# Half-size products for the last four groups of an input projection, PSUM banks 6 and 2, stores on two queues

## The chip, the cores and the metric

The kernel runs on one core of a Trainium2 chip. The metric is the device time of one execution in microseconds (us); lower is better. Five engines work side by side: TensorE (PE, matrix products), VectorE (DVE), ScalarE (ACT), GpSimd (POOL) and SyncE (SP, which here only issues DMA transfers). An engine runs its instructions in order; an instruction that waits for another engine holds up all that stands behind it on its own.

## The reference, cut to what matters

One encoder layer over a sequence of 2048 positions and 2048 channels, in float32:

```python
h = rms_norm(x, norm_g) * (1 + scale) + shift            # scale, shift, gate from silu(c) @ w_ada
z = h @ w_in + b_in                                      # 2048 x 2048 @ 2048 x 4096: input projection
u_pool, u_lru, g_pool, g_lru = z[:, :1024], z[:, 1024:2048], z[:, 2048:3072], z[:, 3072:]
y_pool = pool_mixer(u_pool, ...)                         # 4 groups of 256 channels: window sums, then a 256 x 256 product
y_lru = bidir_rg_lru(conv(u_lru), ...)                   # 4 heads of 256 channels: gate products, a scan in each direction
y = concat(rms_norm(y_pool) * silu(g_pool), rms_norm(y_lru) * silu(g_lru)) @ w_out + b_out   # output projection
out = rms_norm(x + gate * y, final_norm_g)
```

## The kernel before

**Steps.** The program is a loop over steps `t`. A step is 24 matmuls of 128x128 by 128x512 (line 310): each of four output banks of 128x512 gets 256 rows of the contraction, and each float32 product is made of three products of split operands (`mm3`: high by high, high by low, low by high). Step `t` has a moving tile `m` (the split of a raw tile of 128x2x512 floats, made by ACT and DVE two steps ahead in `m_split`, lines 169 and 170) and a stationary tile `s`.

**Stages.** Steps 0 to 255 are the input projection: eight groups (four "L" heads, four "P" pool groups) of four blocks of 512 positions, eight steps a block. After a block ACT moves its four banks out of PSUM (`evac`, line 449): two to the group's `u` tiles in SBUF, two to a raw tile `gr`, which is stored to DRAM. Steps 256 to 367 are the output projection, in two halves of 56 steps. Each half is a 2 by 2 block product made of seven products of half size instead of eight (Strassen's way in Winograd's form): sums and differences of blocks are multiplied (`PRODUCTS`), and the results are added up in `out_evac`. The differences of the moving side (`T1` to `T4`, out of `w_out`) are made ahead by `combine` and kept in DRAM; those of the stationary side are made in `unit_split`.

**Work beside the steps.** The units of the groups (`lru_unit`: convolution, gate products on PE, sigmoid, scan, merge; `pool_unit`: window sums, product, gating) are put at steps by the tables `L_START` and `P_START`; their products use the banks `px`. All else (the 48 rows of `w_ada`, `combine`, row norms, final rows) is put at steps by `at`. A scheduler then orders each engine's instructions within narrow bounds; an engine's order is fixed when the program is built.

**Buffers.** PSUM has eight banks: five `pm` for the projections, three `px` for all else (in the output projection every second block takes three `px` and one `pm`). Raw tiles of 512 KB rotate through eight buffers (`raw_p`): a load into one waits until the tile that was handed out eight earlier is done with. Eight `s` buffers hold stationary tiles, three hold moving tiles, eight `big` ones hold `u` tiles and others. SP issues all loads and stores, in order (`load`, `store`).

Of the kernel before, what the change touches and what calls it, by code (L numbers as in the profile page):

```python
# [13 lines left out]
D = 2048  # L14
S = 2048
# [29 lines left out]
def layer(ctx: ExitStack, tc: tile.TileContext, xc, xn, c, wada, win, wgate, wpool, wout, vecs, consts, bout, fng, out):  # L45
# [3 lines left out]
    s_p = pool("s", 8)  # L49
# [7 lines left out]
    ps_m = pool("ps_m", 5, space=bass.MemoryType.PSUM)  # L57
    ps_x = pool("ps_x", 3, space=bass.MemoryType.PSUM)
# [45 lines left out]
    sscr = [dram.tile([128, 2, TB], F32, name=f"ss{p}") for p in range(4)]  # L104
# [28 lines left out]

    def wout_src(name, p, q):
        k = int(name[1:])
        if name[0] == "T":
# [38 lines left out]
    def modulate(t):  # L175
# [10 lines left out]
        store(out=xscr[tb][p], in_=r)  # L186
# [91 lines left out]
    def normed(r, sg, h, k, p):  # L278
        for j in range(2):
            vtt(out=r[:, j], in0=r[:, j], in1=rn_t[2 * sg + h, "PL"[k]], op=ALU.mult)  # L280
        late.append((yscr[PAIRS[p + 4 * k]][2 * sg + h], r))
        if (sg, h, p) == (0, 1, 3):
            del rn_t[1, "PL"[k]], rn_t[0, "PL"[k]]

    def unit_split(u):
# [16 lines left out]
        s = s_p.tile([128, 2, 2, TB], F32R, tag="s", name="s")  # L302
# [132 lines left out]
    def evac_fix(g, tb):  # L435
# [5 lines left out]
        store(out=gscr[g][tb], in_=gr)  # L441

    def evac(g, tb, banks):
# [6 lines left out]
        store(out=gscr[g][tb], in_=gr)  # L450
# [32 lines left out]
    def lru_unit(g, h, d, tb, b, last):  # L483
# [48 lines left out]
        def scan():  # L532
# [21 lines left out]
            if d == 0:  # L554
                store(out=hscr[h][tb], in_=st["h"])
# [486 lines left out]
```

## Time and profile before

| | before |
|---|---|
| median of 3 runs | 2274.55 us (2274.26 to 2274.68) |
| profiled execution: time, span | 2274.88 us, 2272.7 us |
| PE busy | 2241.9 us, 9832 matmuls |
| DVE, ACT busy | 1656.3 us, 1294.4 us |
| data moved | 533.55 MB, mean 235 GB/s |

The span is the time from the first instruction to the last as the profiler saw it; the profiled execution's own time is 2.18 us longer. A busy time is the union of an engine's instructions. A PE that waits inside a row of matmuls can be shown as busy, so matmuls are also counted by stretch. "Idle before" is an engine's waiting time ahead of a group of instructions, with what ended it.

### The profile page before, as it was taken

The numbers are of one execution on the slowest core, as the hardware profiler recorded it, in microseconds if no ns is written. First come the engines' busy times: TensorE is split into PE (matmuls) and PEld (weight loads), VectorE is DVE, ScalarE is ACT, GpSimd is POOL, SyncE is SP. The second block draws the span as 40 slices with busy tenths as digits, with TensorE's granted clock in tenths as the row PEclk, the third lists the DMA queues.
The fourth block names the chain that finished last, engine by engine and source line by source line (L and its number), as shares of the span: only waits on it lengthen the run. The fifth ranks groups of instructions, "written<-read, shape, count | busy, mean of one in ns | idle before, by whom it ended". The sixth has DMA issues, their size and how long they took to land.

```text
span 2272.7 us, 26096 instructions
## 1 busy us (share of the span) xinstructions
PE 2241.9 (99%) x9832; PEld 1845.5 (81%) x9832; DVE 1656.3 (73%) x1986; ACT 1294.4 (57%) x1609; POOL 6.2 (0%) x40
## 2 busy tenths in 40 slices
PE   7999999999999999999999999999999999999996
PEld 6888888888888888888888888887788888888885
DVE  7999677478867564677675657668976668977579
ACT  4555677576755666666667467678643333443332
POOL 0000000000000000000000000000000000000000
PEclk9999999999999999999999999999999999999998
DMA  9878766445956654674466446654787657897555
GB/s 390 330 281 334 262 218 225 178 158 202 342 184 235 241 180 172 213 245 158 168 251 238 176 171 228 233 200 168 268 306 277 216 192 241 318 364 259 187 177 203
DMA packets 139455, 533.55 MB, mean 235 GB/s; under 512 B 15424, under 2 KB 16704, under 8 KB 131392
## 3 DMA queue, kind: packets, MB, share of 16 engines
q1 hardware_dynamic: 139328, 531.88, 65.1%
q8 instruction: 77, 1.26, 0.2%
q14 instruction: 50, 0.41, 0.1%
HBM read 417.52 MB, written 114.29 MB: 234 GB/s over the span
## 4 chain that ended last, share of the span: by engine, by line
PE 95%; DVE 3%; DMA 1%; issue 0%; ACT 0%; SPq 0%; DVEq 0%
PE pm L310 75%; PE px L310 20%; DVE o L775 1%; DMA ada<-in_wada_dram 1%; DMA xr<-in_xc_dram 0%; PE px L393 0%; DVE sqP L395 0%; DVE m L170 0%; DVE o L754 0%; DVE o L753 0%; DVE sqL L395 0%; DVE o L725 0%; PE px L707 0%; DVE x L746 0%; DVE th L549 0%
## 5 line engine op out<-in xcount | busy, mean ns | idle before, releaser
L310 PE MATMUL pm<-m,s 128*128 128x512 f32 x7674 | 1771.0, 390 | 0.0
L310 PEld LDWEIGHTS pm<-m,s 128*128 128x128 f32 x7674 | 1440.8, 188 | 304.0 <-issue 4.1
L169 ACT ACTIVATE m<-xr 128x1024 fp32r<-128x1024 f32 x366 | 386.4, 1056 | 587.0 <-PE pm L310 396.8
L170 DVE TENSOR_TENSOR m<-xr,m 128x1024 fp32r<-128x1024 f32 x366 | 446.2, 1219 | 359.8 <-ACT m L169 348.1
L310 PE MATMUL px<-m,s 128*128 128x512 f32 x1134 | 270.7, 392 | 13.8 <-ACT m L359 12.4
L310 PEld LDWEIGHTS px<-m,s 128*128 128x128 f32 x1134 | 213.6, 189 | 60.3 <-ACT m L359 12.4
L310 PE MATMUL px<-uch,gw 128*128 128x512 f32 x768 | 186.8, 391 | 0.0
L310 PEld LDWEIGHTS px<-uch,gw 128*128 128x128 f32 x768 | 144.3, 188 | 31.5 <-ACT sqL L394 0.5
L378 DVE CUSTOM_DVE_ANT_0 ada<-ada,cact 128x2048 f32<-128x2048 f32 x47 | 107.4, 2285 | 11.7 <-DMA ada<-in_wada_dram 11.7
L520 DVE TENSOR_TENSOR ig<-ig,u 128x512 f32<-128x512 f32 x64 | 44.1, 689 | 58.7 <-ACT ig L518 58.7
L303 ACT ACTIVATE s<-yr 128x1024 fp32r<-128x1024 f32 x56 | 59.0, 1053 | 46.3 <-DVE yr L299 21.8
L539 DVE SCALAR_TENSOR_TENSOR th<-rg,th 128x512 f32<-128x512 f32 x64 | 42.5, 683 | 51.7 <-ACT th L534 51.3
L304 DVE TENSOR_TENSOR s<-yr,s 128x1024 fp32r<-128x1024 f32 x56 | 68.2, 1218 | 12.3 <-ACT s L303 12.2
L235 DVE TENSOR_TENSOR s<-wr,s 128x1024 fp32r<-128x1024 f32 x56 | 68.1, 1215 | 1.0 <-ACT s L234 1.0
L185 ACT ACTIVATE xr<-xr,shv 128x512 f32<-128x512 f32 x64 | 44.3, 719 | 34.2 <-DVE xr L184 29.5
L755 ACT ACTIVATE x<-o 128x1024 f32<-128x1024 f32 (+1 forms) x36 | 34.7, 965 | 50.6 <-DVE o L754 49.1
L234 ACT ACTIVATE s<-wr 128x1024 fp32r<-128x1024 f32 x56 | 58.6, 1046 | 3.8 <-PE pm L310 2.0
L504 ACT ACTIVATE uch<-u 128x512 fp32r<-128x512 f32 x64 | 38.8, 626 | 37.3 <-DVE u L499 37.2
L253 DVE TENSOR_TENSOR tr<-tr 128x1024 f32<-128x1024 f32 x32 | 39.1, 1221 | 22.3 <-DMA tr<-in_wout_dram 21.3
L518 ACT ACT_TABLE_LOAD x42 | 53.9, 1283 | 0.7
L499 DVE SCALAR_TENSOR_TENSOR cv<-u,vec,cv 128x512 f32<-128x512 f32 x64 | 45.8, 743 | 6.7 <-ACT cv L497 6.7
L518 ACT ACTIVATE ig<-px,vec 128x512 f32<-128x512 f32 x64 | 43.7, 683 | 10.7 <-PE px L310 10.2
(161 smaller groups left out, 1658.3 us busy)
## 6 DMA issues: line engine op xcount, KB each, us to landing
xr<-xs SPq DMA_DIRECT2D x192, 512.0 KB, 5.4
ada<-in_wada_dram SPq DMA_DIRECT2D x47, 1024.0 KB, 6.9
yr<-ys SPq DMA_DIRECT2D x88, 512.0 KB, 4.7
wr<-in_win_dram SPq DMA_DIRECT2D x71, 512.0 KB, 6.0
xr<-t SPq DMA_DIRECT2D x64, 512.0 KB, 4.4
xr<-in_xc_dram SPq DMA_DIRECT2D x63, 512.0 KB, 6.3
tr<-in_wout_dram SPq DMA_DIRECT2D x48, 512.0 KB, 4.7
xr<-in_wout_dram SPq DMA_DIRECT2D x48, 512.0 KB, 4.7
```

The costliest lines, as they stand in the source:

```text
L169: act(out=m[:, 0], in_=r, func=AF.Copy)
L170: vtt(out=m[:, 1], in0=r, in1=mf[:, 0], op=ALU.subtract)
L185: act(out=r[:, j], in_=r[:, j], func=AF.Identity, bias=shv[:, k:k + 1])
L234: act(out=s[:, 0], in_=r, func=AF.Copy)
L235: vtt(out=s[:, 1], in0=r, in1=sf[:, 0], op=ALU.subtract)
L303: act(out=s[:, 0], in_=r, func=AF.Copy)
L304: vtt(out=s[:, 1], in0=r, in1=s.bitcast(F32)[:, 0], op=ALU.subtract)
L310: nc.tensor.matmul(out=ps, lhsT=a[:, x, j, asl], rhs=b[:, y, j], start=first and i == 0, stop=last and i == 2, skip_group_check=more)
L378: nc.vector.tensor_tensor_reduce(out=t, in0=t, in1=cact["t"], op0=ALU.mult, op1=ALU.add, scale=1.0, scalar=0.0, accum_out=mod[:, i:i + 1])
L499: stt(out=a if k < 3 else U[i][:, us], in0=src, scalar=cw, in1=a, op0=ALU.mult, op1=ALU.add)
L518: act(out=v, in_=st.pop(("ps", w, i)), func=AF.Sigmoid, bias=V("b_gate", (d * 4 + h) * 4 + 2 * w + i))
L520: vtt(out=st["i", i], in0=st["i", i], in1=U[i][:, us], op=ALU.mult)
```

## The change

Steps 128 to 255 of the input projection (its last four groups) become 112 steps: two supergroups `sg` 0 and 1 of two groups each, every one made of seven half-size products like the output projection. The output projection is now `sg` 2 and 3, and the program has 352 steps. The order of groups 4 and 5 is swapped, and the columns of `w_in` are laid out accordingly.

- `combine` runs for both projections: 32 differences of blocks of the normalised input (`xscr`) go to `hcomb` at steps 66 to 138, 32 of `w_out` to `tscr` at steps 138 to 233.
- `unit_split` makes the stationary sums for all four supergroups; `S2` now stores two tiles (`sscr[0]`, `sscr[1]`), so `S3` needs no subtraction.
- `in_evac` adds up the seven products of the input projection, mostly on DVE straight from PSUM, in `u` and two `sum` tiles; `evac` stays for groups 1 to 3.
- Product 1 is chained onto product 0 in the same banks (and 6 onto 5) only in `sg` 3; in `sg` 2 that sum is made by DVE in `out_evac`.
- PSUM: six `pm` banks and two `px`. `s` tiles: six, and two more (`sx`) up to step 128; from there the space holds the `sum` tiles.
- Stores of `modulate` and `evac` are issued by ACT (`act_store`); `hscr`, `yscr`, `gscr` and `tscr` stores go through the list `late`, which SP issues at the next step, after that step's loads.
- The unit tables (`L_AT`, `P_AT`), the loads of final rows and the norms are put at other steps.

```diff
-GROUPS = [("L", 0), ("P", 3), ("L", 1), ("L", 2), ("P", 2), ("L", 3), ("P", 1), ("P", 0)]
+GROUPS = [("L", 0), ("P", 3), ("L", 1), ("L", 2), ("L", 3), ("P", 2), ("P", 1), ("P", 0)]
...
-    s_p = pool("s", 8)
+    s_p = pool("s", 6)
...
-    ps_m = pool("ps_m", 5, space=bass.MemoryType.PSUM)
-    ps_x = pool("ps_x", 3, space=bass.MemoryType.PSUM)
+    last_p = {"p": tc.alloc_tile_pool(name="sx", bufs=2)}
+    ps_m = pool("ps_m", 6, space=bass.MemoryType.PSUM)
+    ps_x = pool("ps_x", 2, space=bass.MemoryType.PSUM)
...
+    act_store = nc.scalar.dma_start
...
-    NT1 = 256
+    T1 = 128
     SG = 56
+    NT1 = T1 + 2 * SG
     NT = NT1 + 2 * SG
...
-        store(out=xscr[tb][p], in_=r)
+        act_store(out=xscr[tb][p], in_=r)
...
-        store(out=gscr[g][tb], in_=gr)
+        act_store(out=gscr[g][tb], in_=gr)
...
+    def in_evac(sg, k, q, banks):
...
+            if k == 0:
+                act(out=hi, in_=ps, func=AF.Copy)
+            elif k == 1:
+                stt(out=lo, in0=ps, scalar=bu, in1=hi, op0=ALU.add, op1=ALU.add)
+            elif k == 2:
+                vtt(out=hi, in0=ps, in1=hi, op=ALU.add)
+            elif k == 3:
+                vtt(out=U3[q][:, n], in0=ps, in1=hi, op=ALU.add)
+            elif k == 4:
...
+                stt(out=g_t[g, q][:, i], in0=U3[q][:, n], scalar=bg_, in1=ps, op0=ALU.add, op1=ALU.subtract)
...
+            elif k == 5:
+                stt(out=U3[q][:, n], in0=ps, scalar=bg_, in1=U3[q][:, n], op0=ALU.add, op1=ALU.add)
+                vtt(out=hi, in0=ps, in1=hi, op=ALU.add)
...
+            else:
+                stt(out=hi, in0=ps, scalar=bu, in1=hi, op0=ALU.add, op1=ALU.add)
...
-            store(out=yscr[g][tb], in_=gr)
+            late.append((yscr[g][tb], gr))
...
+            more = sg == 3 and k in CHAINED
+            key = (8 + sg, CHAINED[k] if more else k, q)
...
-                banks[key] = [px(), px(), px(), pm()] if t >= NT1 and q else [pm() for _ in range(4)]
+                banks[key] = [px(), px(), pm(), pm()] if t >= T1 and sg == 3 and q else [pm() for _ in range(4)]
```

What this does to the queues is shown at three places. First, the end of a block of the input projection. Before, ACT copies the four banks (`u_...` and `gr` from `pm`), here in the third group:

```order
L449 ACTIVATE u_3381<-pm,vec 128x512
L449 ACTIVATE u_3384<-pm,vec 128x512
L449 ACTIVATE gr<-pm,vec 128x512 x2
L169 ACTIVATE m<-xr 128x1024 x3
L518 ACT_TABLE_LOAD
```

Now, in the second half of the input projection, DVE does it; here the sixth product of `sg` 0 (k = 5, q = 0), with the moving tile's split (L180) ahead:

```order
L180 TENSOR_TENSOR m<-xr,m 128x1024
L608 SCALAR_TENSOR_TENSOR th<-rg,carry,ig 128x512
L504 SCALAR_TENSOR_TENSOR sum<-pm,vec,sum 128x512
L505 TENSOR_TENSOR u_6662<-pm,u_6662 128x512
L504 SCALAR_TENSOR_TENSOR sum<-pm,vec,sum 128x512
L505 TENSOR_TENSOR u_6665<-pm,u_6665 128x512
L504 SCALAR_TENSOR_TENSOR sum<-pm,vec,sum 128x512
L505 TENSOR_TENSOR u_6668<-pm,u_6668 128x512
L504 SCALAR_TENSOR_TENSOR sum<-pm,vec,sum 128x512
L505 TENSOR_TENSOR u_6671<-pm,u_6671 128x512
L626 TENSOR_TENSOR hl<-hl,th 128x512 x2
```

The reading of the banks has moved from ACT to DVE, and at this product it is eight instructions instead of four. Second, SP's queue in the third group. Before, the stores of `gr` and `hf` stand between the loads of moving tiles (`xr`):

```order
L154 DMA xr<-xs_3_229 128x1024
L555 DMA hs_0_138<-hf 128x1024
L154 DMA xr<-xs_4_230 128x1024
L154 DMA xr<-xs_5_231 128x1024
L450 DMA gs_0_114<-gr 128x1024
L154 DMA xr<-xs_6_232 128x1024
```

Now the store of `gr` is issued by ACT, and SP has the loads and stores of the differences (`tr`, `h_...`) instead:

```order
L164 DMA xr<-xs_5_262 128x1024
L1017 DMA hs_1_142<-hf 128x1024
L269 DMA tr<-h_1_0_227 128x1024
L269 DMA tr<-xs_5_262 128x1024
L164 DMA xr<-xs_6_263 128x1024
L164 DMA xr<-xs_7_264 128x1024
L269 DMA tr<-h_1_1_228 128x1024
L269 DMA tr<-xs_5_270 128x1024
L164 DMA xr<-xs_0_265 128x1024
L1017 DMA h_1_0_243<-tr 128x1024
```

The store that waits for a block's end has left SP's queue, and up to three other transfers stand between two loads of moving tiles. Third, PE early in the input projection, around the gate products of an L unit (`px<-uch,gw`), which come in two halves of 12. Before:

```order
L310 MATMUL px<-uch,gw 128x512 x12
L310 MATMUL pm<-m,s 128x512 x24
L310 MATMUL px<-uch,gw 128x512 x12
L310 MATMUL pm<-m,s 128x512 x120
```

Now:

```order
L334 MATMUL px<-uch,gw 128x512 x6
L334 MATMUL pm<-m,s 128x512 x18
L334 MATMUL px<-uch,gw 128x512 x6
L334 MATMUL pm<-m,s 128x512 x106
L334 MATMUL px<-uch,gw 128x512 x12
```

With two `px` banks a half fills both, so the next half needs both of them read; in some places the scheduler has put 18 matmuls of a step between the two products of a half.

## Rows read from the trace of the kernel before

**Rows 1.** The page: busy us (share) and instructions; the granted clock by slice.

```profile
PE 2241.9 (99%) x9832; PEld 1845.5 (81%) x9832; DVE 1656.3 (73%) x1986; ACT 1294.4 (57%) x1609; POOL 6.2 (0%) x40
...
PEclk9999999999999999999999999999999999999998
```

**Rows 2.** The page: the chain that ended last, by engine.

```profile
PE 95%; DVE 3%; DMA 1%; issue 0%; ACT 0%; SPq 0%; DVEq 0%
```

**Rows 3.** PE in order of time: start us, us, what, count [idle before].

```profile
12.38 3.96 PE L310 MATMUL px<-m,s 128*128 128x512 f32 x9 [12.38 <-ACT m L359]
...
2254.41 1.56 PE L310 MATMUL pm<-ml,s 128*128 128x512 f32 x6
```

**Rows 4.** Groups by form: names, shapes, count | busy us, mean ns | idle before, releaser.

```profile
L310 PE MATMUL pm<-m,s 128*128 128x512 f32 x7674 | 1771.0, 390 | 0.0
...
L170 DVE TENSOR_TENSOR m<-xr,m 128x1024 fp32r<-128x1024 f32 x366 | 446.2, 1219 | 359.8 <-ACT m L169 348.1 <-DMA gwr<-in_wgate_dram 6.5 <-DMA gl<-gs 4.3
L169 ACT ACTIVATE m<-xr 128x1024 fp32r<-128x1024 f32 x366 | 386.4, 1056 | 587.0 <-PE pm L310 396.8 <-issue 150.9 <-DMA xr<-in_wout_dram 10.2
L310 PE MATMUL px<-m,s 128*128 128x512 f32 x1134 | 270.7, 392 | 13.8 <-ACT m L359 12.4 <-DVE m L170 0.7 <-ACT s L364 0.5
...
L304 DVE TENSOR_TENSOR s<-yr,s 128x1024 fp32r<-128x1024 f32 x56 | 68.2, 1218 | 12.3 <-ACT s L303 12.2
...
L303 ACT ACTIVATE s<-yr 128x1024 fp32r<-128x1024 f32 x56 | 59.0, 1053 | 46.3 <-DVE yr L299 21.8 <-DVE yr L280 10.7 <-DVE yr L296 9.4
...
L253 DVE TENSOR_TENSOR tr<-tr 128x1024 f32<-128x1024 f32 x32 | 39.1, 1221 | 22.3 <-DMA tr<-in_wout_dram 21.3 <-DMA tr<-t 0.8 <-issue 0.2
...
L449 ACT ACTIVATE u<-pm,vec 128x512 f32<-128x512 f32 x56 | 37.1, 680 | 11.6 <-PE pm L310 11.5
...
L299 DVE TENSOR_TENSOR yr<-yr 128x1024 f32<-128x1024 f32 x16 | 19.5, 1221 | 15.5 <-DMA yr<-ss 9.1 <-DMA yr<-ys 6.4
...
L725 DVE TENSOR_TENSOR o<-pm,o 128x512 f32<-128x512 f32 x20 | 13.1, 684 | 3.6 <-PE pm L310 3.5
```

**Rows 5.** The chain in order of time: start us, us, what.

```profile
297.67 27.21 PE pm L310 x120
```

**Rows 6.** Stretches: us, length, busy (count) by engine, clock, DMA share, GB/s.

```profile
0.00:60.00 60.00, 46.87 (x197) 37.87 (x198) 48.39 (x62) 27.92 (x32) 0.44 (x6) 1.00 0.99 391
120.00:180.00 60.00, 60.00 (x262) 49.00 (x261) 59.94 (x86) 34.04 (x37) 0.00 (x0) 1.00 0.87 329
...
660.00:720.00 60.00, 60.00 (x266) 49.67 (x265) 40.86 (x48) 35.51 (x45) 0.00 (x0) 1.00 0.52 190
...
1920.00:1980.00 60.00, 60.00 (x266) 49.73 (x265) 59.46 (x68) 25.87 (x38) 0.00 (x0) 1.00 0.82 293
1980.00:2040.00 60.00, 60.00 (x266) 49.69 (x266) 46.11 (x48) 22.81 (x29) 0.00 (x0) 1.00 0.97 364
```

**Rows 7.** The same for steps 88 to 95, and for steps 128 to 255.

```profile
543.03:597.78 54.75, 54.75 (x241) 44.94 (x240) 48.96 (x65) 46.20 (x58) 0.28 (x4) 1.00 0.83 299
...
799.28:1637.81 838.53, 838.28 (x3675) 689.37 (x3674) 561.23 (x701) 554.18 (x685) 0.83 (x12) 1.00 0.58 205
```

**Rows 8.** Waits of SP's queue: who waited for whom, us, times, longest us.

```profile
SPq L450 <- ACT gr L449: 181.8, 26, 19.7
SPq L154 <- DVE m L170: 157.0, 53, 10.1
```

**Rows 9.** The page: DMA issues by form, count, KB each, median us to landing.

```profile
xr<-xs SPq DMA_DIRECT2D x192, 512.0 KB, 5.4
```

**Rows 10.** ACT around one L unit's first gate products, in order of time.

```profile
736.55 0.69 ACT L518 ACTIVATE rg<-px,vec 128x512 f32<-128x512 f32 x1
737.14 0.68 ACT L518 ACTIVATE ig<-px,vec 128x512 f32<-128x512 f32 x1
```

**Rows 11.** PE at the same place.

```profile
736.66 5.61 PE L310 MATMUL pm<-m,s 128*128 128x512 f32 x24
742.11 2.89 PE L310 MATMUL px<-uch,gw 128*128 128x512 f32 x12
```

More of the change, by code (lines that the diff above doesn't have):

```diff
@@ L156, in m_load @@
             sg, k, q, p = where2(t)
-            load(out=r, in_=wout_src(PRODUCTS[k][1], p, q))
+            load(out=r, in_=moving("in" if sg < 2 else "out", PRODUCTS[k][1], p, q))
         xraw[t] = r
@@ L554, in scan @@
             if d == 0:
-                store(out=hscr[h][tb], in_=st["h"])
+                late.append((hscr[h][tb], st["h"]))
         def reload():
@@ L650, in fin @@
                 vtt(out=v, in0=v, in1=y, op=ALU.add)
-            store(out=yscr[g][tb], in_=gr)
+            late.append((yscr[g][tb], gr))
         at(b, sums)
@@ L731, in out_evac @@
                 vtt(out=b[:, hi], in0=ps, in1=b[:, hi], op=ALU.add)
+                if not sg:
+                    vtt(out=a[:, hi], in0=ps, in1=a[:, hi], op=ALU.add)
     x_t = {}
@@ L736, in row_of, with x_pair @@
         return 8 * sg + n
+    def x_pair(sg, n):
+        t = big("x")[:, :D].rearrange("p (i t) -> p i t", i=2)
+        i = row_of(sg, n)
+        for k in range(2):
+            load(out=t[:, k], in_=xn[(i + k) * 128:(i + k + 1) * 128, 1024:])
+            x_t[sg, n + k, 1] = t[:, k]
     def x_load(sg, n, h):
@@ L863, in start_unit, with rn_load, rn @@
             pool_unit(g, GROUPS[g][1], tb, b, last)
-    rn_at = [(244, 1, "L"), (244, 2, "L"), (245, 3, "L"), (245, 0, "P"), (249, 1, "P"), (250, 0, "L"), (254, 2, "P"), (259, 3, "P")]
+    def rn_load(tb, kind):
+        r = raw("rq")
+        load(out=r, in_=qscr[kind][tb])
+        rn_t[tb, kind] = r
+    def rn(tb, kind):
+        if "rn" not in fin:
+            fin["rn"] = big("rn")[:, :4 * TB].rearrange("p (i t) -> p i t", i=4)
+        r = rn_t[tb, kind]
+        v = rn_t[tb, kind] = fin["rn"][:, 2 * (tb % 2) + (kind == "L")]
+        ps = px()
+        vtt(out=r[:, 0], in0=r[:, 0], in1=r[:, 1], op=ALU.add)
+        nc.tensor.matmul(out=ps, lhsT=ones, rhs=r[:, 0], start=True, stop=True)
+        act(out=v, in_=ps, func=AF.Sqrt, scale=2.0 / S, bias=epsc)
+        nc.vector.reciprocal(out=v, in_=v)
+    rn_at = [(228, 0, "P"), (229, 0, "L"), (230, 1, "L"), (231, 2, "L"), (232, 3, "L"), (242, 1, "P"), (248, 2, "P"), (254, 3, "P")]
     def rn(tb, kind):
@@ L922, in layer @@
             sg, k, q, p = where2(t)
-            key = (8 + sg, CHAINED.get(k, k), q)
+            more = sg == 3 and k in CHAINED
+            key = (8 + sg, CHAINED[k] if more else k, q)
             sk = (8 + sg, PRODUCTS[k][0])
-            first, last = p == 0 and k not in CHAINED, p == 3
+            first, last = p == 0 and not more, p == 3
+        e = t + W_AHEAD - 25
+        if 0 <= e < 96 and e % 32 < 8:
+            w_load(e // 32 + 1, e % 32)
+        if t + W_AHEAD in unit_at:
+            unit_load(unit_at[t + W_AHEAD])
         for dst, src in late:
@@ L948, in layer @@
             if t == 0:
-                banks[key] = [px(), px(), px(), pm()]
+                banks[key] = [px(), px(), pm(), pm()]
             else:
-                banks[key] = [px(), px(), px(), pm()] if t >= NT1 and q else [pm() for _ in range(4)]
+                banks[key] = [px(), px(), pm(), pm()] if t >= T1 and sg == 3 and q else [pm() for _ in range(4)]
         bk = banks[key]
         if t < NT - 4:
-            step(bk, sk, p, M_t.pop(t), range(4), first, last, t == 0, t >= NT1 and k in CHAINED)
-        if t < NT - 4 and (t >= NT1 and q or t < NT1 and tb == 3):
+            step(bk, sk, p, M_t.pop(t), range(4), first, last, t == 0, t >= T1 and more)
+        if t < NT - 4 and (q if t >= T1 else tb == 3):
             del S_t[sk, p]
         if last:
-            if t < NT1 or k not in CHAINED.values():
+            if t < T1 or sg < 3 or k not in CHAINED.values():
                 del banks[key]
@@ L996, in _lay_out @@
         cols += [slice(u, u + 256), slice(2048 + u, 2048 + u + 256)]
-    w = np.concatenate([w_in[0][:, s] for s in cols], axis=1)
+    order = cols[:8] + [cols[8 + 4 * s + k] for s in range(2) for k in (0, 2, 1, 3)]
+    w = np.concatenate([w_in[0][:, s] for s in order], axis=1)
     a["win"] = w.reshape(8, 2, 128, 8, 512).transpose(3, 0, 2, 1, 4)
```

212 lines of the change are left out of this document (119 added, 93 removed).

## The prediction

> **What bounds the kernel now.** I read the page's busy times first: PE is busy 99% of the span, DVE 73%, ACT 57%, and the granted clock stands at its upper level in all slices but the last [rows 1]. A busy PE can hide waiting, so the chain of work that ended last comes next: 95% of it is PE, and neither a DMA nor another engine holds more than 3% [rows 2]. In order of time, PE's first matmul starts at 12.38 us and its last ends at 2254.41 + 1.56 = 2255.97 [rows 3]; 16.7 us of row sums, scaling and stores follow. Of 13.8 us that PE is seen waiting ahead of these matmuls, 12.4 are the start [rows 4]. A run of 120 matmuls takes 27.21 us, 0.2268 each [rows 5], so a step of 24 takes 5.44; a free stretch of 60 us holds 60 / 0.2268 = 264.6 of them, and the trace counts 262 to 266, even where DVE is busy 59.9 of 60 us [rows 6]. PE is the bound from 12 to 2256 us, and nothing else reaches the path for more than a few us.
>
> **What it removes.** 128 of the 368 steps become 112. That is 16 x 24 = 384 matmuls at 0.2268 us = **87.1 us** off PE. Gate products, pool products and norms on PE stay in number. Start and tail keep their work: the last 16 us hold the same final rows. The profiled execution took 2274.88 us, 2.18 above its span and 0.33 above the median; so the sum without any new wait is 2274.88 - 87.1 = **2187.8**, or 2187.5 beside the median. Everything below asks how much of the 87.1 is lost again.
>
> **What it adds on DVE.** In-place sums from PSUM: per supergroup 8 banks for each of seven products, product 0 on ACT, product 5 with two operations: 56 x 2 = 112 at 0.684 (as the reading of `pm` at line 725) = 76.6. Splits of stationary tiles: 56 units for 32 loaded ones, 24 x 1.218 = 29.2. Sums for S2, S1, S4: 32 x 1.221 = 39.1. `combine` for the input: 32 x 1.221 = 39.1. Away: S3's subtraction in the output, 8 x 1.221 = 9.8, and 16 moving splits, 16 x 1.219 = 19.5. The unchained pairs of `sg` 2: 16 x 0.684 = 10.9. Sum +166 us [rows 4]. 1656 + 166 = 1822 of some 2190 us, 83%: not a bound as a mean. By stretches of eight steps (instructions as the order has them, durations of before; durations overlap, their sum in before is 1747 for 1656 busy, so 5% off) DVE has about 55 us of work against 54 of PE in steps 80 to 87, 50 against 57 in 184 to 191, 49 against 50 in 224 to 231, and stays below nine tenths in most others. Before had such stretches and hid them: 59.94 of 60 us busy from 120 to 180 us, 59.46 from 1920 to 1980, with 262 (four of them slow norm matmuls) and 266 matmuls [rows 6]. Moving tiles are split two steps ahead, so DVE may fall behind by some 9 us before PE waits. By my count the backlog peaks at 9 us around step 32 (8 before), 8 at step 172 and 8 at step 232, where five reciprocals and product 5 meet. Cost taken: 1 us; the ends are 0 and, if nothing of it were covered, 166. Without the cover, the next late thing is the moving tile, and PE waits for DVE's split.
>
> **ACT.** It loses 64 evictions (0.68) and 16 moving copies (1.06) and gains 24 stationary copies (1.05) and 16 plain evictions: about 43.5 + 16.9 less 25.3 + 10, a relief of 25 us [rows 4]. It takes on 44 stores to issue; at the 0.3 to 0.4 us that SP's issues last this is some 15 us, in steps 29 to 127, where moving copies, sigmoids and table loads stand behind it. ACT is busy 46 of 55 us in its fullest such stretch [rows 7], so 0 is taken; uncovered it would be 15.
>
> **SP's queue.** The stores that ACT takes were the worst heads of it: SP waited 181.8 us in 26 waits for the end of a block, up to 19.7 us with all loads standing behind [rows 8]. PE lost nothing by that, so nothing is gained but slack. The stores that are now late wait for DVE one step later and behind that step's loads: 0.
>
> **Two px banks.** A unit's second gate half now needs both banks of the first half read. Where little goes on, ACT has read them at 737.14 + 0.68 = 737.82 and PE needs them at 742.11 [rows 10, 11]: 4.3 us to spare, cost 0. Where a stationary copy or a sum of two tiles stands ahead in ACT's queue (1.05 to about 3.4 us), the spare time is nearly used up. At the other end, a wait of a table load and two reads (2.6 us) at each of 32 units is 85 us, all of the gain. I stay near the row: 3 us. The six pm banks: the next product's third bank needs the oldest bank read within two banks' work, 12 matmuls = 2.7 us, after its step; DVE does so unless it is 5 us late at that step, which I find nowhere: 0, at worst 2.7 us at 28 products, 76.
>
> **Raw buffers.** By names in the order, steps 128 to 239 hand out 318 raw tiles in 720 us of PE time, 18.1 us of life for each of eight buffers; steps 192 to 199 leave 14.3, and 216 to 223 only 12.3. The tightest stretch before, steps 88 to 95, had 25 tiles in 54.75 us, 17.5 us each, and lost nothing (241 matmuls in 54.75 us) [rows 7]. That SP waits for a moving split to free a buffer so often, 53 times for one group of loads [rows 8], says that buffers are taken as early as they are free, so a shorter life mostly eats lead. A load lands in 5.4 us [rows 9] and takes 1.06 + 1.22 to be split [rows 4], 8 to 9 us with gaps; one that is stored again needs some 14. Cost taken: 3 us around step 220.
>
> **Forecast.** 2187.8 + 1 + 3 + 3 = 2194.8, less 0.3 to the median: **2194.5**, faster by 80 us.
>
> **Rivals.** (a) *Banks and buffers bind in the half-size input stage.* For it: two px instead of three, reading on the fuller engine, stretches with 12 to 14 us per raw buffer where before had 17.5. Against it: slack of 4.3 us at the only place that the trace shows, lead of two steps. If a quarter to three quarters of the 85 us of px waiting appear: 2209 to 2251. (b) *Transfers bind.* In steps 120 to 127 some 39 transfers of 512 KB (20.5 MB) meet 49 us, and as many meet 43.5 us in steps 304 to 311; the fullest slice of the trace moved 391 GB/s at a share of 0.99 [rows 6], by which they take 52.4 us: 3.4 + 8.9 = 12 us late, 2200 if no neighbour absorbs it. The Trainium skill, in "DMA: Bandwidth & Descriptors", section "Where 436 GB/s comes from", says that between HBM and SBUF a core's share of HBM, some 358 GB/s, binds; by it five stretches overrun (8.2, 3.7, 3.9, 2.1 and 13.7 us), an estimate of 32 us and a time of 2219. Two slices of this trace, at 391 and 364 GB/s, lie above that figure, so the measurement decides against it. (c) *Slower.* One mechanism: the life of a raw buffer in the stage's 112 steps. Loads go out in order, so once a mean life exceeds 18.1 us every step is stretched in proportion. The gain is gone, with 0.2% more, at (720 + 87 + 5) x 8 / 318 = 20.4 us. For it: tiles that are stored again, and `gr` and `hf`, live longest, and SP's waits of up to 20 us [rows 8] can pass from tile to tile; at a life of 21 us the kernel takes 2303. Against it: lives of 17.5 us were lived with before, and most tiles are loads whose lead can shrink by half. That the change does not do what it says is out: the order has 352 x 24 matmuls of this line.
>
> **How the numbers follow.** Forecast, with waits of 0 to 15 us: 2187 to 2203, chance 0.70. (b) 0.08, 2200 to 2219. (a) 0.17, 2205 to 2251, mostly in its lower half. (c) 0.05. A range from 2187 to 2222 leaves out (c) and the upper part of (a), about 0.15. A measurement of this kernel can tell some 0.2%, 4.5 us, from no change. Slower is (c) without its mild forms, 0.04; no change needs a loss of 82 to 92 us and has 0.02; faster has 0.94.
>
> **What would show it.** Right: 9408 matmuls of the split kind at 0.227 us; PE's waits, the start apart, in single us; the last matmul near 2176; DVE busy near 1820 and ACT near 1265. If a stretch of the stage from some 815 to 1535 us has under 262 matmuls in 60 us, a step of the above is wrong: PE released by ACT's sigmoid reads says px; by DVE sums from `pm`, the six banks; by a moving split behind a DMA, raw buffers or transfers; by a moving split behind DVE work, DVE's backlog. My forecast is wrong above all if such waits repeat at each unit, since then a few us each come 16 to 32 times.

## The result, and the profile after

The changed kernel takes **2220.0 us** (median of 4 runs, 2217.1 to 2224.2) against 2274.6 before: 0.976 of it, 95% interval 0.974 to 0.978. Forecast were 2194.5 us and a gain of 80 us; measured are 54.6. The time lies near the upper end of the range (2187 to 2222) and outside the likeliest case's own (2187 to 2203), so the question of this part is where some 25 us went. Of the prediction's cases with a price only (a) has a range that holds 2220, and the waits that it priced, for `px` banks, did not occur; that the time still lies inside 2187 to 2222 is partly luck. The profiled execution took 2217.4 us.

The page after, as [rows 1] and [rows 2]:

```profile
PE 2166.2 (98%) x9448; PEld 1775.4 (80%) x9448; DVE 1802.0 (81%) x2178; ACT 1255.3 (57%) x1552; POOL 6.2 (0%) x40
...
PEclk9999999999999999999999999999999999999999
...
PE 29%; DVE 5%; DMA 4%; issue 1%; ACT 1%; SPq 0%; DVEq 0%; ACTq 0%
```

PE still looks 98% busy. The chain tells more, but its shares add up to only some 40%: followed back from the end, it breaks off at 1333.39 us. In the part that it covers PE has 29 of 40, some seven tenths, where before it had 95 of 100; the rest lies with DVE and with transfers. PE's first and last row, as [rows 3]:

```profile
12.39 2.95 PE L334 MATMUL px<-m,s 128*128 128x512 f32 x6 [12.39 <-ACT m L383]
...
2200.17 1.52 PE L334 MATMUL pm<-ml,s 128*128 128x512 f32 x6
```

From the start of one to the end of the other it is 54.3 us less than before; the tail behind is 13.7 us, before 16.7. So -87.1 for the 384 matmuls, -3.0 for the tail, and **+32.7 of new losses** in between make -57.4; the span shrank by 57.3. PE's own waits name the first part of these (who waits for whom: us, times, longest):

```profile
PE px L334 <- ACT m L383: 12.4, 1, 12.4
PE pm L334 <- DVE sum L788: 7.9, 2, 4.1
PE px L334 <- ACT uch L563: 5.2, 4, 2.8
PE px L334 <- DVE uch L564: 4.2, 7, 1.3
PE px L334 <- ACT uch L687: 3.7, 2, 2.2
```

The first is the start. No row names ACT's sigmoid reads of `px` (L577), so the two `px` banks are not it. What is waited for is the sum of product 1 in the first output half (L788, which DVE makes out of `pm`), and the split of the units' moving tile `uch` (lines 563, 564, 687), made by ACT and DVE one step ahead of its product. Stretches, columns as [rows 6]:

```profile
0.00:60.00 60.00, 46.98 (x196) 37.90 (x197) 48.26 (x62) 27.79 (x32) 0.44 (x6) 1.00 0.98 391
120.00:180.00 60.00, 60.00 (x263) 48.94 (x262) 59.94 (x86) 34.08 (x37) 0.00 (x0) 1.00 0.88 329
780.00:840.00 60.00, 57.19 (x246) 46.81 (x245) 53.65 (x64) 40.00 (x49) 0.48 (x8) 0.97 0.92 337
1620.00:1680.00 60.00, 52.12 (x214) 41.87 (x214) 47.35 (x55) 27.22 (x33) 0.00 (x0) 0.93 0.79 269
1900.00:1960.00 60.00, 60.00 (x266) 49.71 (x265) 51.62 (x57) 25.43 (x37) 0.00 (x0) 1.00 0.87 314
```

A stretch with DVE at 59.94 of 60 us still holds 263 matmuls, four of them of a norm. Those with too few (246 and 214) have a granted clock under 1.00 as well: PE stands, and then runs slowly.

**A late load and what stands behind it.** The worst place of the input stage is step 129. SP:

```profile
822.24 0.32 SPq L1017 DMA_DIRECT2D ys<-gl  x1
822.65 2.78 SPq L167 DMA_DIRECT2D xr<-xs  x2
825.68 0.96 SPq L296 DMA_DIRECT2D yr<-in_win_dram  x1
```

Why SP came to these loads so late is told by its waits from 806.5 to 826 us:

```profile
SPq L269 <- DVE m L180: 11.8, 2, 6.8
SPq L1017 <- DVE gl L628: 2.2, 1, 2.2
SPq L167 <- DVE m L180: 2.0, 1, 2.0
```

In 13.8 of these 19.5 us the next load (L269, L167) had no free buffer until DVE had split an older moving tile (L180); 2.2 us it stood at the store `ys<-gl`, which waited for DVE.

ACT at the same place, with its idle time and what ended it:

```profile
828.41 1.06 ACT L179 ACTIVATE m<-xr 128x1024 fp32r<-128x1024 f32 x1 [3.79 <-DMA xr<-xs]
833.39 1.06 ACT L327 ACTIVATE s<-yr 128x1024 fp32r<-128x1024 f32 x1 [3.92 <-DMA yr<-in_win_dram]
834.35 1.13 ACT L563 ACTIVATE uch<-u 128x512 fp32r<-128x512 f32 x2
```

And PE:

```profile
835.02 0.72 PE L334 MATMUL px<-uch,gw 128*128 128x512 f32 x2 [2.81 <-ACT uch L563]
```

PE needs neither the `m` nor the `s` of these rows at once; they are made ahead. But ACT works in order, and `uch`, which has nothing to do with either load, stands behind both. PE waits 2.81 us for it, at 835.02.

**The entrance to the output projection** (steps 248 to 263). DVE:

```profile
1666.03 1.29 DVE L301 TENSOR_TENSOR yr<-yr,sqP 128x512 f32<-128x512 f32 x2 [3.24 <-DMA yr<-ys]
1668.55 0.69 DVE L301 TENSOR_TENSOR yr<-yr,sqL 128x512 f32<-128x512 f32 x1 [1.23 <-DMA yr<-ys]
...
1670.30 0.68 DVE L788 TENSOR_TENSOR sum<-pm,sum 128x512 f32<-128x512 f32 x1
1670.90 1.22 DVE L319 TENSOR_TENSOR yc<-yr 128x1024 f32<-128x1024 f32 x1
1672.03 3.35 DVE L419 RECIPROCAL sqP<-sqP 128x512 f32<-128x512 f32 x1
1675.29 1.16 DVE L328 TENSOR_TENSOR s<-yc,s 128x1024 fp32r<-128x1024 f32 x1
1676.37 0.68 DVE L788 TENSOR_TENSOR sum<-pm,sum 128x512 f32<-128x512 f32 x1
```

DVE stands 4.5 us at late `yr` tiles, then a reciprocal of 3.35 us comes between the first and second reading of the product's banks, and PE, out of `pm` banks, waits 3.76 us until 1677.10. It had waited 4.12 us for the sum of this line 32 us before:

```profile
1644.78 4.51 PE L334 MATMUL pm<-m,s 128*128 128x512 f32 x12 [4.12 <-DVE sum L788]
...
1677.10 11.50 PE L334 MATMUL pm<-m,s 128*128 128x512 f32 x39 [3.76 <-DVE sum L788]
```

The granted clock is lower after both:

```profile
1644.78:1649.10 4.32, 4.32 (x12) 3.48 (x13) 4.32 (x6) 0.24 (x1) 0.00 (x0) 0.63 0.93 339
1677.10:1679.40 2.30, 2.30 (x5) 1.82 (x6) 2.30 (x4) 0.00 (x0) 0.00 (x0) 0.50 1.02 420
1679.40:1690.00 10.60, 10.60 (x41) 8.27 (x40) 8.36 (x11) 4.63 (x5) 0.00 (x0) 0.87 1.02 412
```

After the wait five matmuls take 2.30 us, 0.46 each: the lower of the two levels, 1.2 GHz. At 0.2268 us per matmul these three stretches lose 1.6, 1.2 and 1.3 us, 4 us on top of 7.9 us of waiting.

### The profile page after: what moved, and what is told of

It is laid out like the page before. It is cut to its first block, busy times and chain, and to the rows that moved or that the text cites. A ratio compares the mean times of both kernels' runs of the same rounds, so it can differ in the third digit from the quotient of the medians.

```text
span 2215.4 us, 25700 instructions
## 1 busy us (share of the span) xinstructions
PE 2166.2 (98%) x9448; PEld 1775.4 (80%) x9448; DVE 1802.0 (81%) x2178; ACT 1255.3 (57%) x1552; POOL 6.2 (0%) x40
## 5 line engine op out<-in xcount | busy, mean ns | idle before, releaser
L334 PE MATMUL pm<-m,s 128*128 128x512 f32 x8004 | 1857.8, 391 | 7.9 <-DVE sum L788 7.9
L334 PEld LDWEIGHTS pm<-m,s 128*128 128x128 f32 x8004 | 1506.3, 188 | 330.7 <-DVE sum L788 8.7
L180 DVE TENSOR_TENSOR m<-xr,m 128x1024 fp32r<-128x1024 f32 x350 | 426.9, 1221 | 131.9 <-ACT m L179 125.2
L327 ACT ACTIVATE s<-yr 128x1024 fp32r<-128x1024 f32 x104 | 109.5, 1054 | 92.3 <-DMA yr<-in_win_dram 27.1
L328 DVE TENSOR_TENSOR s<-yr,s 128x1024 fp32r<-128x1024 f32 x104 | 126.9, 1221 | 22.3 <-ACT s L327 22.3
L334 PE MATMUL px<-m,s 128*128 128x512 f32 x420 | 105.0, 394 | 13.0 <-ACT m L383 12.4
L402 DVE CUSTOM_DVE_ANT_0 ada<-ada,cact 128x2048 f32<-128x2048 f32 x47 | 107.4, 2288 | 10.4 <-DMA ada<-in_wada_dram 10.4
L274 DVE TENSOR_TENSOR tr<-tr 128x1024 f32<-128x1024 f32 x64 | 78.3, 1224 | 45.3 <-DMA tr<-xs 16.9
L334 PEld LDWEIGHTS px<-m,s 128*128 128x128 f32 x420 | 79.1, 190 | 30.6 <-ACT m L383 12.4
L334 PE MATMUL px<-uch,pw 128*128 128x512 f32 x192 | 50.0, 398 | 5.1 <-ACT uch L687 3.7
L577 ACT ACTIVATE ig<-px,vec 128x512 f32<-128x512 f32 x64 | 43.8, 684 | 15.5 <-PE px L334 15.1
L577 ACT ACTIVATE rg<-px,vec 128x512 f32<-128x512 f32 x64 | 43.9, 686 | 12.7 <-PE px L334 12.3
L194 DVE SCALAR_TENSOR_TENSOR xr<-xr,sc,rl 128x512 f32<-128x512 f32 x64 | 45.5, 750 | 6.9 <-DMA xr<-in_xc_dram 6.9
```

The source lines that it names most:

```text
L180: vtt(out=m[:, 1], in0=r, in1=mf[:, 0], op=ALU.subtract)
L194: stt(out=r[:, j], in0=r[:, j], scalar=sc[:, k:k + 1], in1=rr, op0=ALU.mult, op1=ALU.mult)
L327: act(out=s[:, 0], in_=r, func=AF.Copy)
L328: vtt(out=s[:, 1], in0=r, in1=s.bitcast(F32)[:, 0], op=ALU.subtract)
L334: nc.tensor.matmul(out=ps, lhsT=a[:, x, j, asl], rhs=b[:, y, j], start=first and i == 0, stop=last and i == 2, skip_group_check=more)
L402: nc.vector.tensor_tensor_reduce(out=t, in0=t, in1=cact["t"], op0=ALU.mult, op1=ALU.add, scale=1.0, scalar=0.0, accum_out=mod[:, i:i + 1])
```

## The losses, stage by stage

The table gives, for the profiled execution of each run (all described below), the time between first matmuls of steps in PE's rows, less the time that the matmuls between them need (0.22675 us each, those of a norm 0.88). Of before, the stages are steps 0 to 71, 72 to 143, 144 to 255, 256 to 263 and 264 to 367. The last columns: the sum of ACT's and DVE's wait rows that name a DMA, and the median with its range.

| run | 0-71 | 72-143 | 144-247 | 248-263 | 264-351 | sum | at a DMA | us (range) |
|---|---|---|---|---|---|---|---|---|
| before | 3.7 | 1.1 | 2.4 | 0.3 | 1.0 | 8.5 | 170 | 2274.6 |
| after | 4.2 | 11.0 | 13.8 | 12.3 | -0.1 | 41.2 | 280 | 2220.0 (2217.1-2224.2) |
| e1 | 3.9 | 12.5 | 19.2 | 8.4 | 0.0 | 44.0 | 253 | 2219.2 (2217.5-2224.6) |
| e2 | 3.8 | 16.8 | 34.5 | 6.1 | 1.8 | 63.0 | 300 | 2240.7 (2237.1-2246.0) |
| e3 | 4.2 | 29.7 | 52.3 | 8.2 | 18.3 | 112.7 | 399 | 2290.5 (2288.6-2296.4) |
| e4 | 3.6 | 10.4 | 25.5 | 8.9 | -0.1 | 48.3 | 272 | 2223.2 (2220.0-2225.8) |
| e5 | 3.6 | 8.7 | 9.3 | 5.5 | 5.7 | 32.8 | 190 | 2210.3 (2208.2-2216.5) |
| e6 | 4.0 | 6.4 | 22.2 | 7.6 | 0.1 | 40.3 | 238 | 2217.8 (2213.2-2220.2) |
| e7 | 34.6 | 14.6 | 18.4 | 10.1 | -0.1 | 77.6 | 354 | 2258.4 (2256.3-2260.1) |
| e8 | 7.2 | 10.8 | 17.7 | 9.4 | -0.1 | 45.0 | 279 | 2222.3 (2221.2-2224.4) |
| e9 | 3.9 | 15.7 | 24.5 | 5.1 | -0.1 | 49.1 | 288 | 2220.0 (2216.6-2225.6) |
| e10 | 3.7 | 20.4 | 19.2 | 10.3 | -0.1 | 53.5 | 286 | 2230.5 (2228.7-2233.6) |
| e11 | 3.7 | 12.5 | 10.7 | 2.4 | 3.0 | 32.3 | 178 | 2207.4 (2206.6-2208.3) |
| e12 | 4.7 | 6.7 | 16.5 | 1.7 | 4.5 | 34.1 | 190 | 2216.1 (2210.1-2218.9) |

A stage must be read against its own spread. Steps 144 to 247 are not touched in e1, e6, e7, e8, e9 (to step 241) and e10; with the changed kernel itself they lose 14 to 25 us there. Steps 72 to 143 lose 11 to 16 us untouched (after, e1, e7, e9), steps 248 to 263 8 to 12 us (after, e6, e7, e8, e10). Only what leaves these bands says something.

The scheduler also orders each engine's instructions anew for every kernel. Counted by names in the traces, e7 and e10 have the order of after, and in e1, e4 and e9 at most 28 of DVE's 2178 instructions stand elsewhere; in e6 and e8 it is some 100, but at least 248 do in e2, 272 in e3, 293 in e5, 307 in e11 and 392 in e12, and on ACT 90 to 160. Those five runs change the order together with what their edit says, and no run here separates the two. (e11 differs from e5 by only 26 and 2.)

## The experiments

Two theories on the 32.7 us: A, PE loses them where DVE reads `pm` banks late; C, raw buffers decide when loads start, and late loads hold ACT and DVE ahead of what PE needs. Against them stand B (DVE has too much work of its own), D (buffers have lead to spare), E (stores at the head of SP's queue make loads late) and F (transfers are the bound).

**e1: product 1 out of `pm` by ACT.**

```diff
-                vtt(out=a[:, lo], in0=ps, in1=a[:, hi], op=ALU.add)
+                act(out=a[:, lo], in_=ps, func=AF.Copy)
+                vtt(out=a[:, lo], in0=a[:, lo], in1=a[:, hi], op=ALU.add)
```

> Product 1 of the first output half (steps 248 to 255) is moved out of its banks by ACT, and DVE adds afterwards from SBUF. Theory A (the changed kernel's waits in steps 248 to 263, some 8 us of waiting and 4 us at a lower granted clock, come from six pm banks that DVE reads late): both waits go, 2220 - 10 = 2207 to 2212 us, and PE's waits for a DVE sum from pm fall from 7.9 us to under 2. Rival B (DVE simply has too much work there): the wait moves to a split of a moving tile or to the next product's sums, 2216 us or more. ACT takes on 16 evictions of 0.68 us and DVE the same sums from SBUF.

Measured 2219.2 us, ratio 0.976 (0.974 to 0.978): no gain. The waits at L788 are gone, and PE waits somewhat later for DVE all the same, at the diagonal tile of the gate rows. PE, then DVE:

```profile
1689.55 2.07 PE L770 MATMUL px<-dg,ones 128*128 128x512 f32 x2 [4.66 <-DVE dg L767]
```

```profile
1668.57 1.29 DVE L301 TENSOR_TENSOR yr<-yr,sqP 128x512 f32<-128x512 f32 x2 [3.47 <-DMA yr<-ys]
...
1688.62 0.87 DVE L767 TENSOR_SCALAR dg<-cst,gcol 128x128 f32<-128x128 f32 x4
```

So theory A alone falls: the banks are only where DVE's lateness first meets PE. B's "wait moves" holds, with a late load ahead of DVE here too.

**e2: seven raw buffers.**

```diff
-    raw_p = pool("raw", 8)
+    raw_p = pool("raw", 7)
```

> Seven raw buffers instead of eight. Theory C (in the half-size input stage and just before it, the life of a raw buffer sets when loads start, and late loads hold ACT and DVE ahead of the units' splits; about 20 us are lost by it): life falls from some 18 to 15.5 us, and the loss doubles or triples, 2240 to 2275 us. Rival D (buffers have lead to spare; loads are late because a store at the head of SP's queue holds them, or because transfers are slow): under 8 us more, 2220 to 2228 us.

Measured 2240.7 us: 20.6 more, the lower end of C and far outside D. The loss in steps 144 to 247 is 34.5 us, outside its band. That the number of buffers sets when loads go out can be read directly: in steps 128 to 239 the load of a moving tile is issued 25.7 us ahead of its step at the mean with seven buffers, 28.4 with eight, 30.5 with nine (e5), 35.3 in before; the load of a stationary tile, in steps 144 to 247, 9.5, 12.7 and 15.3 us ahead of the step at which it is split.

**e3: late stores on GpSimd's queue.**

```diff
-            store(out=dst, in_=src)
+            nc.gpsimd.dma_start(out=dst, in_=src)
```

> The stores of the late list (differences, y, h, g tiles) are issued by GpSimd's queue, which is idle, instead of SP's, so that no load stands behind a store that waits for DVE. Theory E (those stores at the head of SP's queue make loads late; SP waits some 220 us for them): most of the 20 us lost in steps 72 to 208 come back, 2198 to 2208 us. Theory C (buffers set it, a load behind a store would find no free buffer anyway): 2216 to 2224 us.

Measured 2290.5 us, 70 us more, slower than before (ratio 1.007, 1.006 to 1.009); neither theory had that. GpSimd's queue stands for up to 25 us in these rows:

```profile
449.53 0.53 POOL L1017 DMA_DIRECT2D ys<-gl  x1 [24.81 <-DVE gl L628]
453.61 0.53 POOL L1017 DMA_DIRECT2D h<-tr  x1 [3.54 <-DVE tr L274]
...
486.71 0.54 POOL L1017 DMA_DIRECT2D ys<-gl  x1 [25.03 <-DVE gl L628]
```

But it holds up nothing that is ready. All 64 stores of differences go out within 0.42 us of DVE's sum (by SP in after up to 9.84 us behind it), and they have landed 7.0 us after the sum at the median, in after 8.1. What changes is where SP waits: it no longer stands at these stores and instead comes to buffers whose stores have not landed. In steps 128 to 239 its loads wait 283 us for stores to land; in after it was 90, and 148 at the stores themselves. Two of SP's rows of e3, and the same two of after:

```profile
SPq L296 <- DMA t<-tr: 49.3, 8, 7.1
SPq L164 <- DMA h<-tr: 46.7, 8, 8.9
```

```profile
SPq L296 <- DMA t<-tr: 6.5, 3, 2.6
SPq L164 <- DMA h<-tr: 6.4, 3, 4.0
```

Theory E as it was put falls: with these stores aside and sooner out, no time comes back. Why 70 us are lost is open. Moving tiles' loads even go out earlier than in after (31.2 us ahead of their step for 28.4, steps 128 to 239), while in steps 72 to 263 ACT and DVE stand 72 us at `tr` tiles for 38 and 50 at `gl` tiles for 20; the order of the engines differs as well, and a store of `h<-tr` lands 6.8 us after its issue, by SP 6.0. Nor does the run clear such stores: in after SP stood 6.6 us at a store `ys<-yr`, up to 1635.2 us, with loads behind it.

**e4: banks five and three again**, in `pm` and `px` and in the two lines that hand out mixed sets.

```diff
-    ps_m = pool("ps_m", 6, space=bass.MemoryType.PSUM)
-    ps_x = pool("ps_x", 2, space=bass.MemoryType.PSUM)
+    ps_m = pool("ps_m", 5, space=bass.MemoryType.PSUM)
+    ps_x = pool("ps_x", 3, space=bass.MemoryType.PSUM)
```

> Five pm banks and three px, as in the kernel before, with the rest of the change. If two px banks cost something (rival a of the prediction), time falls to 2210 to 2216 us. If not, and Theory A holds (pm banks read late by DVE), one bank less makes these waits longer and more frequent: 2226 to 2245 us, with PE waiting for DVE sums from pm well over the 7.9 us of the changed kernel.

Measured 2223.2 us, ratio 0.977 (0.976 to 0.979), not to be told from after. The edit gives one bank and takes another, so it tests the sum of both. As after has no wait for a `px` bank, a third has nothing to give there, and a `pm` bank less then costs little; A's second half falls as well.

**e5: nine raw buffers.** The room comes from two scratch tiles and from the vector tile.

```diff
-    raw_p = pool("raw", 8)
+    raw_p = pool("raw", 9)
...
-    ... for n, b in (("tmp", 9), ("gw", 1), ("uch", 1))]
+    ... for n, b in (("vec", 1), ("tmp", 7), ("gw", 1), ("uch", 1))]
...
-    vec = one.tile([128, NV], F32, name="vec")
+    vec = vec_p.tile([128, NV], F32, name="vec")
```

> Nine raw buffers. The room for it comes from seven scratch tiles (tmp) instead of nine and from placing the vector tile where its room is used again after step 255. Theory C (the life of a raw buffer sets when loads start): the first buffer taken away cost 20 us, the one added gives back a third to two thirds of the 33 us that the changed kernel lost: 2198 to 2212 us. Rival F (transfers, not buffers, are slow): 2217 to 2224 us. If the two scratch tiles are missed, the time rises above 2224.

Measured 2210.3 us, ratio 0.972 (0.971 to 0.974), 9.7 less than after: inside C's range, outside F's. In the profiled execution all three stages from 72 to 263 lie below their bands, 13.6 us less than after together. But steps 264 to 351, without loss in after, lose 5.7: near the end DVE's split of a moving tile (L180) stands behind sums of final rows, and PE waits 3.67 us for it, until 2172.91. The other two kernels with nine buffers, e11 and e12, wait 2.7 us at the same place. Two of ACT's wait rows for moving tiles, of after, then the first of them in e5; the second has no counterpart there (a row names the transfer that the profile saw land last; what a split of `m` reads is `xr`):

```profile
ACT m L179 <- DMA yr<-ys: 17.5, 4, 4.4
...
ACT m L179 <- DMA xr<-t: 12.9, 3, 4.3
```

```profile
ACT m L179 <- DMA yr<-ys: 4.4, 1, 4.4
```

PE waits 3.0 us for L788 instead of 7.9, though nothing about that product was changed. What the two scratch tiles and the new order did to this was not measured.

**e6: no differences for the input.** `combine` stays for the output only; T1 to T4 read plain blocks.

```diff
-        for proj, b in (("in", 66 + i * 9 // 4), ("out", 138 + 3 * i)):
+        for proj, b in (("out", 138 + 3 * i),):
```

> Left out: the differences of the moving side for the input projection; 64 loads, 32 sums and 32 stores of steps 66 to 138 go, and the products T1 to T4 take plain blocks instead. PE's work is the same. Theory C: the loss of steps 72 to 143 (some 13 us) falls to 2 or 3, what is lost from step 144 on (some 20 us) stays: 2205 to 2212 us. If the combining costs nothing there: 2216 us or more.

Measured 2217.8 us, 2.2 less, with overlapping intervals: the expectation of 2205 to 2212 missed. Steps 72 to 143 do lose less, 6.4 against 11 to 16 us, but not the 10 expected. By this one execution 96 transfers and 39 us of DVE there cost PE some 5 to 9 us.

**e7: transfers without a buffer, first try.**

```diff
         late.append((moving(proj, f"T{k + 1}", p, q), a))
+        if proj == "in":
+            i = 4 * k + p
+            nc.gpsimd.dma_start(out=xtra[i % 8], in_=xn[128 * i:128 * i + 128, 0:1024])
```

> One transfer of 512 KB from DRAM to DRAM more at each of the 32 combinations of the input (steps 68 to 138), issued by GpSimd, without any buffer in SBUF. Rival F (transfers bind there): 16.8 MB at 391 GB/s are 43 us of 16 DMA engines, of which 15 us or more appear: 2235 to 2262 us. Theory C: transfers have room there (277 GB/s on average), landing is a little later, 0 to 10 us more: 2218 to 2230 us.

Measured 2258.4 us, but not for the reason asked: these transfers wait for nothing but each other, and GpSimd issued them in the first 120 us, not at steps 68 to 138 (its instructions are in the fifth pair of the rows).

```profile
0.00:60.00 60.00, 29.52 (x102) 22.90 (x103) 27.71 (x38) 17.20 (x20) 10.38 (x25) 0.91 0.98 375
60.00:120.00 60.00, 52.00 (x196) 41.27 (x196) 44.05 (x50) 22.09 (x26) 7.03 (x17) 0.86 1.02 401
```

It shows what bound transfers look like: a share of 0.98 to 1.02 for 120 us, and 16.8 MB more cost 30 us in steps 0 to 71.

**e8: the stores of ACT on SP again.**

```diff
-    act_store = nc.scalar.dma_start
+    act_store = nc.sync.dma_start
```

> The 44 stores of the normalised input and of the g blocks are issued by SP again, as in the kernel before, in place of ACT. If SP's waiting for them at the head of its queue makes loads late (raw buffers then have less lead than before): 2224 to 2240 us. If ACT's 15 us of issuing is what made ACT late: 2210 to 2217 us. The prediction took either as nothing: 2217 to 2224 us.

Measured 2222.3 us, ratio 0.977 (0.976 to 0.979), 2.3 more than after with overlapping intervals. That part of the change is worth nothing that can be measured here, as the prediction took it.

**e9: three reciprocals left out** (steps 242, 248, 254).

```diff
-        nc.vector.reciprocal(out=dst, in_=dst)
+        if inverse:
+            nc.vector.reciprocal(out=dst, in_=dst)
```

> Left out: the reciprocals of three norms of the pool half (positions 512 to 2047) at steps 242, 248 and 254, 3 x 3.35 us of DVE. If DVE's own backlog makes the 12 us lost in steps 248 to 263 (Theory B), 8 us or more come back there: 2208 to 2213 us, and PE's waits for DVE sums from pm fall from 7.9 us to under 2. If late loads of y tiles, at which DVE stands, make them (Theory C), at most 4 us come back: 2216 us or more.

Measured 2220.0 us: no gain in the median, as C had it; but the loss of steps 248 to 263 is 5.1 us, below its band of 8 to 12, as B had it. The two don't contradict each other: the profiled execution, at 2225.6, is the slowest of the four, and lost 40 us in the untouched stages before. Of a gain of 3 to 7 us the median can show none with this spread. Undecided by itself; with e5 and e11 it suggests that late loads and DVE's own work both have a part.

**e10: the extra transfers in their place**, each a copy of the difference just stored.

```diff
+        for src in again:
+            copies.append(0)
+            nc.gpsimd.dma_start(out=xtra[len(copies) % 8], in_=src)
+        again.clear()
```

> The extra transfers of the run before, this time each behind the store of its difference (512 KB out of h into a scratch block, DRAM to DRAM, by GpSimd; steps 69 to 140). Nothing else changes and no buffer in SBUF is used. Rival F (transfers bind in steps 72 to 143): 15 us or more on top, 2235 to 2262 us. Theory C: 0 to 8 us on top by later landing, 2217 to 2230 us.

Measured 2230.5 us, 10.4 more: between the two theories. The stretch from 440 to 820 us (some steps 72 to 127), first of after, then of e10:

```profile
440.00:820.00 380.00, 376.35 (x1650) 308.83 (x1649) 311.80 (x395) 272.35 (x342) 0.76 (x12) 1.00 0.82 298
```

```profile
440.00:820.00 380.00, 371.92 (x1616) 303.04 (x1615) 303.53 (x386) 263.74 (x333) 11.69 (x31) 1.00 0.88 324
```

The queues have room on average (0.82 and 0.88), and the 43 us of transfers cost a quarter of what they last, where at the start they cost 30. So transfers are not the bound, but not free either: each buffer is held while its data travels (median landing of `xr<-xs` in this stretch 5.7 us after, 6.3 in e10). Both expectations missed, C's by 0.5 us. F as the bound, with 15 us or more, is not borne out; it stays as a part of a buffer's life.

**e11: nine buffers, and DVE relieved at steps 248 to 263**: e5 with the edit of e1, and the diagonal tiles by ACT.

```diff
-            nc.vector.tensor_scalar(out=t[:, j * 128:(j + 1) * 128], in0=cst[:, 0:128], scalar1=gcol[:, k:k + 1], scalar2=None,
-                                    op0=ALU.mult)
+            act(out=t[:, j * 128:(j + 1) * 128], in_=cst[:, 0:128], func=AF.Copy, scale=gcol[:, k:k + 1])
```

> Nine raw buffers, and DVE relieved at the start of the output projection: product 1 of its first half is read by ACT, and the diagonal tiles of the gate rows are made by ACT. With nine buffers alone, 5.5 us were lost in steps 248 to 263. If buffers and DVE's lateness there are separate causes, the gains add up: 2203 to 2207 us. If the wait only moves to the next reader as it did with eight buffers: 2208 to 2213 us.

Measured **2207.4 us**, ratio 0.970 (0.969 to 0.972): faster than both kernels, 12.6 below after and 67 below before. Steps 248 to 263 lose 2.4 us, where nine buffers alone left 5.5 and e1's half of the relief alone 8.4; what is left there is one wait of 2.1 us for the diagonal tiles, now made by ACT. Against e5 the median is 2.9 less, at the edge of what can be told (the intervals overlap), and between the two expectations. Steps 72 to 143 lose 12.5 us, within their band again, so of e5's three stages the later two are the firm ones.

**e12: the same, stationary loads a step earlier.**

```diff
-    W_AHEAD = 2
+    W_AHEAD = 3
```

> The same, with the loads of stationary tiles one step earlier in SP's queue (three steps ahead instead of two). If ACT and DVE stand at y tiles because these are issued late, 3 to 8 us more come back than in the run before: 2196 to 2204 us. If every buffer is taken as soon as it is free anyway, an earlier place for one tile is a later one for another, and lives get longer: no gain or a loss, 2204 to 2220 us.

Measured 2216.1 us (ratio 0.974, 0.972 to 0.975), 8.7 more than e11: in the second branch's range. Its reason is not shown. The stationary loads did come earlier (in steps 144 to 247 issued 21.7 us ahead of the step of their split, in e11 15.3), and ACT and DVE stood less at them (28 us for 46 in steps 72 to 263); moving tiles kept their lead (30.1 us for 30.7 in steps 128 to 239). The profiled execution, at 2210.1 the fastest of the four, doesn't show what the others lost, and at least 279 of DVE's instructions stand elsewhere than in e11.

## Why the prediction was right, and where it was wrong

- **The 87.1 us: right.** 9408 matmuls of line 334, and the stretches without waits hold 263 to 266 in 60 us as before.
- **DVE and ACT: right in size.** DVE 1802 (forecast 1822), ACT 1255 (1265). DVE's backlog of its own was to cost 1 us at steps 32, 172 and 232: steps 32 to 63 lost 0.8 us, 168 to 175 1.8, 232 to 239 0.6, 3.2 together; whether DVE's backlog is the cause there was not looked into.
- **Two `px` banks, 3 us: nothing** (no wait row, e4). Rival (a) is out on that side, from which its price came; its other half, buffers, is near what was found. **ACT's stores, 0:** holds (e8).
- **Six `pm` banks, 0 us: this step failed.** That PE would wait if DVE read the banks late was right; "which I find nowhere" was not. It is met twice, at 1644.78 and 1677.10, and costs 4.12 and 3.76 us, not 2.7 at worst: 7.9 us of waits, and 4 of lower clock, for which the sum had no term. The count of DVE's work had no late loads in it; DVE stood 6.3 us at `yr` tiles ahead of the first place (3.9 until 1625.8, 2.4 until 1633.9) and 4.5 ahead of the second. e1 shows that the banks are not the cause but the place.
- **Raw buffers, 3 us near step 220: this term was mis-sized.** How much of the other 20 us is its, stays open; e5 and e2 say a good part. Steps 216 to 223 lost 0.3 us; 128 to 135, 184 to 191, 72 to 79 and 88 to 95 lost 4.8, 3.3, 3.0 and 2.7. Two steps of the reasoning fell short. First, a shorter life was to eat the lead of moving tiles. It did (28.4 us for 35.3), and no wait row of PE in after, the start apart, names `m`. But a late load does not only delay its own tile: ACT and DVE stop at it in order, and `uch`, needed one step later, stands behind. Second, for rival (c) life was taken as a property of a tile, so that the stage would stretch in proportion. Steps 128 to 239 take 761, 739 and 732 us with seven, eight and nine buffers. Through the 318 tiles that is 16.8, 18.6 and 20.7 us from one use of a buffer to its next, an average worked out, not a life seen. Had a tile needed the 18.6 us, seven buffers would have made 845 us of the stage: one buffer less costs 3% of it (with the order changed too), not 14%.
- **Rival (b).** The Trainium skill ("DMA: Bandwidth & Descriptors", section "Where 436 GB/s comes from") gave an estimate of 2219 us by its 358 GB/s, and 2220 was measured. It is a coincidence: of the five overruns the prediction places two, and both places lost nothing (steps 120 to 127 0.0 us; 304 to 311 lie in 264 to 351 with -0.1); and the trace moved 412 and 420 GB/s in the rows above, and 401 over 60 us in e7.
- **The tail** was taken as equal and is 3.0 us shorter; why was not looked into.

Shown: with one raw buffer less loads go out later and 20.6 us are lost, with one more they go out earlier and 9.7 come back. That the buffer alone does this, and not the other order of the engines that came with it, is argued and not shown. Some 3 us more with DVE relieved at the entrance to the output projection are likely. Open: e11 still loses 32.3 us where before lost 8.5, with ACT and DVE at a DMA no longer than before (178 against 170 us). In its trace most of PE's remaining waits, 10 of 16 us, are again for `uch`; the longest, 3.23 us until 835.01, is that of step 129 as in after, behind a stationary split on ACT that waited 5.93 us for its load. That this order on ACT alone makes it was only read, not tried.

## What to carry to other kernels

A rotating buffer is not paid for by its own tile alone: ask what stands behind the instruction that waits for the load, on its engine, and how soon PE needs that. Moving loads forward (e12) or stores aside (e3) did what it said here, loads and stores did go out earlier, and the kernel still got slower; only two kernels with one buffer more (e5, e11) got clearly faster. And before a stage of one profiled execution is read as an effect, look at the same stage in runs that don't touch it: here its loss varied by 10 us. Look also whether the scheduler has put the engines' instructions into another order: an edit of one number moved hundreds of them (e2).

## What the runs showed of the hardware

A PE wait can cost more than itself, by what the granted clock does after it. Waits of 1.65 and 2.33 us (e5) left it at 1.00 in the next 10 us; after 2.81 and 3.67 us (after, at 835; e5, at 2173) the mean of the next 10 us was 0.83, after 3.23 us (e11) 0.70, after 4.66 us (e1) 0.75. At 0.83 that is 1.7 us more in 10, at 0.70 3.0. The length of the wait alone does not tell which: after 1.91 us (e9, at 475.34) the mean was 0.83 too, while 2.73 us (e11, at 2173.82) and 2.86 us (e4, at 1685.67) left it at 1.00. A DMA issue takes GpSimd 0.53 us, SP 0.32 and ACT 0.33.
